# Attention in a two-layer hybrid trunk: the halves of a head's output are copied by ScalarE, and added and split for a pair of heads by POOL

## The chip, the cores and the metric

The kernel runs on one core of one Trainium2 chip. The metric is the device time of one execution in microseconds (us). TensorE (PE in the profile, PEld for its weight loads), VectorE (DVE), ScalarE (ACT), GpSimd (POOL) and SyncE (SP) each work through a queue of their own in a fixed order, and wait for one another by semaphores.

## The reference

The model has two layers. Each normalises x, projects it once, runs three mixers side by side (sparse attention with 8 heads, gated linear attention, spatial gating), projects their joined outputs back and adds them to x; a SwiGLU block follows. The sequence is 512 long, the width 1024, a head 64 wide, and everything is in float32. What matters here is the attention mixer:

```python
s = jnp.einsum('bqghd,bcgd->bghqc', qb, kc)                 # 31 compressed blocks
p_cmp = masked_softmax(s, cmp_end <= t)
o_cmp = jnp.einsum('bghqc,bcgd->bqghd', p_cmp, vc)
...
p = masked_softmax(einsum(qb, ksel), tok <= t)              # selected blocks
o_slc = einsum(p, vsel)
...
p = masked_softmax(einsum(qb, kwb), wmask)                  # window
o_win = einsum(p, vwb)
return gb[..., 0:1] * o_cmp + gb[..., 1:2] * o_slc + gb[..., 2:3] * o_win
...
x = x + jnp.concatenate([o_nsa, o_gla, o_sg], axis=-1) @ w_out[l]
```

With 512 positions, 8 blocks of 64 and up to 16 chosen, the second term takes every block, and the window of 512 takes every earlier position. Both are causal attention over the whole sequence, with keys and values of their own.

## The kernel before

To keep float32 precision on matmuls of a rounded type, the kernel splits a value into a high half (the value rounded to that type) and a low half (the rest). A product is then two or three matmuls. Weights are split as they arrive (`w_split`, L318 on ScalarE, L321 on VectorE), tiles read from PSUM or SBUF in `split_psum` (L299 on ScalarE for the high half, L300 on VectorE for the low one).

`mixer` holds a layer's attention. It loops over four pairs of heads (`hp`, from L1188), the two heads of a pair (`hh`), and two branches (`br`: selected and window). For a branch and each of four blocks of 128 queries, TensorE forms scores (L1215, L1216, L1234, L1235), VectorE takes the row maximum (L1218, L1237), and ScalarE the exponential with its row sum (L1222, L1239). The four tiles of P are 128, 256, 384 and 512 columns wide. VectorE turns the sums and the gates into a factor `rr` (L1244, L1245). Then P is scaled by it: the first two tiles on VectorE (L1253), the third on ScalarE (L1251), and the fourth on POOL (L1249), which by a written dependency waits for VectorE's scaling. TensorE transposes P (L1262) in three groups (columns 0, 1, and 2 with 3 of the key blocks); each group is copied out of PSUM as a high and a low half, PT (L299, L300), and multiplied by V (L1275 for the high half of PT, L1276 for the low).

The weights of that last product, `vst`, hold V's high half in 64 columns and its low half in the other 64. So the accumulator O, one PSUM bank of 128 rows by 512 queries, has in 64 rows the product with V's high half and in the other 64 that with V's low half. Both branches and the compressed term (L1286, L1287) add into it, and the head's output is the sum of the two halves of rows. That bank is the only one of its kind (`rings["o"]`), so the first L1275 of the next head waits until O has been read.

At the end of a head, ScalarE copies one half of O to `oc` (L1288), shifted by 64 rows where the half lies in the other half's place, and VectorE adds the other half to it straight from PSUM (L1289). After the second head `oc` has a pair's 128 rows, and `split_psum` makes from it the high and low half that the output projection reads (`kt`, L299 and L300). `oc` comes from a ring of six buffers named tmp.

Nothing in the code writes out the queue order of these steps. A scheduler sets it from the order in the code, from priorities (`tc.high_priority`), and from its own estimate of when inputs are ready. It runs a head's score matmuls and exponentials ahead of the previous head's end. It also fills TensorE's queue within attention with the first half of the output projection (`out_proj` with k0=4, L336 to L338), which needs the other two mixers only.

Of the kernel before, what the change touches and what calls it, by code (L numbers as in the profile page):

```python
# [10 lines left out]
F32 = mybir.dt.float32  # L11
# [5 lines left out]
ALU = mybir.AluOpType  # L17
# [10 lines left out]
H = 8  # L28
# [115 lines left out]
def trunk_kernel(ctx: ExitStack, tc: tile.TileContext, a, out):  # L144
    nc = tc.nc
# [9 lines left out]
    def nm(s):  # L155
        uid[0] += 1
        return f"{s}_{uid[0]}"
# [7 lines left out]
    def psum(tag):  # L165
        taken[tag] += 1
        return banks[:, rings[tag][(taken[tag] - 1) % len(rings[tag])], :]
# [130 lines left out]
    def split_psum(hi, lo, src):  # L298
        nc.scalar.copy(hi, src)  # L299
        nc.vector.tensor_tensor(lo, src, hi.bitcast(F32), op=ALU.subtract)  # L300
# [266 lines left out]
    def mixer(l, norm, xkt, eu=None):  # L567
# [65 lines left out]
        with tc.tile_pool(name=f"mx{l}", bufs=1, reuse_waits="tile") as mp:  # L633
            def tmp(n=SEQ, dt=F32):
                return mp.tile([P, SEQ], dt, tag="tmp", name=nm("tmp"), bufs=6)[:, 0:n]
# [11 lines left out]
            with tc.tile_pool(name=f"ma{l}", bufs=1, reuse_waits="tile") as ap:  # L647
# [29 lines left out]
                for lp in range(2):  # L677
                    hs = slice(64 * lp, 64 * lp + 64)
# [4 lines left out]
                for w_i in range(2):  # L683
                    pa = pos_t(w_i, l).rearrange("p (s a) -> p a s", s=2)
                    for s in range(2):
                        hi, lo = (kvR[w_i][:, :, 65 * s : 65 * s + 1, h] for h in range(2))
# [374 lines left out]
            with tc.tile_pool(name=f"mt{l}", bufs=1, reuse_waits="tile") as tp_:  # L1061
# [20 lines left out]
                for g in range(G):  # L1082
                    for b in range(2):
                        prep_k(g, b)
                    hi = km2[g][64:128].rearrange("p b (n c) -> p b n c", c=P)
# [99 lines left out]
                def load_q(h):  # L1185
                    (nc.gpsimd.tensor_copy if h > 1 else nc.scalar.copy)(qm1[h % GH][0:64], qst[h // GH][0:64, h % GH, :])

                for hp in range(H // 2):  # L1188
                    if hp % 2 == 0:
                        okt[hp // 2] = kt_tile()  # L1190
                    kt = okt[hp // 2]
                    oc = tmp()
                    for hh in range(2):
                        h = 2 * hp + hh
                        g, h4 = h // GH, h % GH
# [5 lines left out]
                        O = psum(OT[h % len(OT)])  # L1201
                        first = True
                        for br in range(2):
# [43 lines left out]
                            for i in SORD:  # L1247
# [4 lines left out]
                                else:  # L1252
                                    scaled = nc.vector.tensor_scalar(ps_[i], ps_[i], rr[:, i : i + 1], None, op0=ALU.mult)  # L1253

                            tc.add_manual_dep(p3.ins, scaled.ins.name, mybir.DependencyInfo(mybir.DependencyClass.Sync, mybir.DependencyReason.DATA),
                                              reason="port")
                            for js in JG:
                                T = psum(TT[js[0]])
                                c = 0
# [24 lines left out]
                        hs = slice(64 * hh, 64 * hh + 64)  # L1284
# [1 line left out]
                        nc.tensor.matmul(O, lhs, pcT[g][0], start=False, stop=False)  # L1286
                        nc.tensor.matmul(O, lhs, pcT[g][1], start=False, stop=True)  # L1287
                        nc.scalar.copy(oc[hs, :], O[ls, :])  # L1288
                        nc.vector.tensor_tensor(oc[hs, :], oc[hs, :], O[hs, :], op=ALU.add)  # L1289
                    split_psum(kt[:, hp % 2, 0, :], kt[:, hp % 2, 1, :], oc)  # L1290
            return okt

    def out_proj(l, okt, k0, kts, nrm, tags=None):
# [413 lines left out]
```

## Time and profile before

| | us |
|---|---|
| median of 3 runs | 1287.74 (1286.69 to 1287.77) |
| the profiled execution | 1286.52 |
| its span, first to last instruction | 1284.7 |
| attention, layer 0 | about 176 to 276 |
| attention, layer 1 | about 806 to 906 |

One execution is profiled on the chip. A row of a group of instructions names the line, the engine, the operation, output and input by the program's names, partitions x elements, the count, the busy time and the mean duration in ns, and the idle time of the engine just before them with what ended it. Matmuls overlap in their pipeline, so a busy PE is not PE at its peak. The rows that carry the argument stand in the prediction.

### The profile page before, as it was taken

Reading aid. Unit: us, or ns where it says so; the run is one execution under the profiler, and the core shown is the slowest. Engines: PE = TensorE matmul, PEld = TensorE weight load, DVE = VectorE, ACT = ScalarE, POOL = GpSimd, SP = SyncE. Lnnn points to the kernel's source line nnn. Section 1 sums busy time; section 2 is a strip of 40 time slices with the busy share of each in tenths; the row PEclk is TensorE's granted clock in tenths of the full one; section 3 lists DMA queues with packets and bytes.
Section 4 is the critical chain, followed back from the end, with each engine's and each line's share of the span. In section 5 each row is a group of like instructions: output and inputs, shape, how many; then the busy total and the mean of one; then the engine's idle time right before and its main releaser. Section 6 shows DMA issues by size and latency. Waiting matters only on the chain. (4 is left out here: it accounts for less than half of the span.)

```text
span 1284.7 us, 18046 instructions
## 1 busy us (share of the span) xinstructions
PE 1257.3 (98%) x6678; PEld 1038.5 (81%) x6678; DVE 918.2 (71%) x1645; ACT 677.0 (53%) x1288; POOL 160.5 (12%) x157
## 2 busy tenths in 40 slices
PE   8999999999999999999999999999999999999997
PEld 7888788778888888888888877777788888888886
DVE  6767799977856775587446678998767457827775
ACT  6675367864533553354346733788544445515532
POOL 0101222122000100010301012121210001000102
PEclk9999999999999999999999999999999999999999
DMA  6451441034335885483434317210533448754811
GB/s 231 142 180 34 115 108 33 17 87 127 98 105 141 197 232 146 111 200 99 115 94 149 116 34 175 64 33 3 146 98 99 131 117 210 216 130 133 227 66 66
DMA packets 134204, 155.01 MB, mean 121 GB/s; under 512 B 9307, under 2 KB 86885, under 8 KB 134117
## 3 DMA queue, kind: packets, MB, share of 16 engines
q1 hardware_dynamic: 117392, 128.81, 33.3%
q0 software_dynamic: 10208, 20.84, 9.2%
q10 hardware_dynamic: 6516, 4.22, 1.5%
q8 instruction: 52, 0.85, 0.3%
q14 instruction: 36, 0.29, 0.1%
HBM read 149.92 MB, written 2.10 MB: 118 GB/s over the span
## 5 line engine op out<-in xcount | busy, mean ns | idle before, releaser
L318 ACT CAST hl<-raw 128x1024 fp32r<-128x1024 f32 (+3 forms) x170 | 175.2, 1035 | 226.5 <-PE banks L338 160.9
L321 DVE TENSOR_TENSOR hl<-raw,hl 128x1024 fp32r<-128x1024 f32 (+3 forms) x170 | 207.1, 1222 | 94.6 <-ACT hl L318 93.0
L336 PE MATMUL banks<-hl,kt 128*128 128x512 f32 (+2 forms) x688 | 257.9, 375 | 1.1 <-ACT hl L318 1.1
L337 PE MATMUL banks<-hl,kt 128*128 128x512 f32 (+2 forms) x688 | 256.4, 373 | 0.0
L338 PE MATMUL banks<-hl,kt 128*128 128x512 f32 (+2 forms) x688 | 256.1, 373 | 0.0
L337 PE MATMUL banks<-kt,hl 128*128 128x512 f32 x384 | 151.5, 394 | 0.0
L338 PE MATMUL banks<-kt,hl 128*128 128x512 f32 x384 | 151.1, 394 | 0.0
L336 PE MATMUL banks<-kt,hl 128*128 128x512 f32 x384 | 150.4, 394 | 0.0
L336 PEld LDWEIGHTS banks<-hl,kt 128*128 128x128 f32 x688 | 129.5, 188 | 23.6 <-ACT hl L318 1.9
L337 PEld LDWEIGHTS banks<-hl,kt 128*128 128x128 f32 x688 | 129.5, 188 | 21.8 <-DVE hl L321 0.3
L338 PEld LDWEIGHTS banks<-hl,kt 128*128 128x128 f32 x688 | 129.4, 188 | 21.7
L318 ACT CAST hl<-wx 128x1024 fp32r<-128x1024 f32 x48 | 50.5, 1052 | 79.8 <-PE banks L338 69.1
L337 PEld LDWEIGHTS banks<-kt,hl 128*128 128x128 f32 x384 | 72.2, 188 | 14.7 <-DVE kt L295 0.9
L338 PEld LDWEIGHTS banks<-kt,hl 128*128 128x128 f32 x384 | 72.3, 188 | 13.7
L336 PEld LDWEIGHTS banks<-kt,hl 128*128 128x128 f32 x384 | 72.0, 188 | 13.3 <-ACT kt L299 0.3
L321 DVE TENSOR_TENSOR hl<-wx,hl 128x1024 fp32r<-128x1024 f32 x48 | 58.7, 1224 | 18.4 <-ACT hl L318 18.2
L500 DVE TENSOR_TENSOR xT<-xT,banks 128x512 f32<-128x512 f32 x56 | 37.5, 681 | 47.6 <-PE banks L338 47.6
L337 PE MATMUL banks<-act,hl 128*128 128x512 f32 x172 | 67.0, 390 | 0.0
L338 PE MATMUL banks<-act,hl 128*128 128x512 f32 x172 | 66.9, 389 | 0.0
L336 PE MATMUL banks<-act,hl 128*128 128x512 f32 x172 | 66.9, 390 | 0.0
L300 DVE TENSOR_TENSOR PT<-banks,PT 128x384 fp32r<-128x384 f32 (+1 forms) x96 | 54.6, 597 | 14.1 <-ACT PT L299 13.2
L336 PE MATMUL banks<-hl,act 128*128 128x512 f32 (+1 forms) x164 | 63.0, 384 | 0.0
(356 smaller groups left out, 2404.1 us busy)
## 6 DMA issues: line engine op xcount, KB each, us to landing
raw<-in_w_gate_dram SPq DMA_DIRECT2D x44, 512.0 KB, 3.9
raw<-in_w_up_dram SPq DMA_DIRECT2D x44, 512.0 KB, 4.0
raw<-in_w_in_dram SPq DMA_DIRECT2D x32, 512.0 KB, 3.7
raw<-in_w_down_dram SPq DMA_DIRECT2D x36, 256.0 KB, 4.0
raw<-in_w_down_dram SPq DMA_DIRECT2D x18, 512.0 KB, 3.7
raw<-in_w_out_dram SPq DMA_DIRECT2D x16, 512.0 KB, 4.3
raw<-in_cmp_w_k_dram SPq DMA_DIRECT2D x8, 512.0 KB, 3.9
raw<-in_cmp_w_v_dram SPq DMA_DIRECT2D x8, 512.0 KB, 4.9
```

The lines of the kernel that those rows point to most:

```text
L300: nc.vector.tensor_tensor(lo, src, hi.bitcast(F32), op=ALU.subtract)
L318: last_cast[:] = [nc.scalar.copy(hl[:, 0, 0:n], raw[:, 0:n])]
L321: e_.tensor_tensor(hl[:, 1, 0:n], raw[:, 0:n], hl[:, 0, 0:n].bitcast(F32), op=ALU.subtract)
L336: nc.tensor.matmul(ps, lh, rh, start=start, stop=False, skip_group_check=skip)
L337: nc.tensor.matmul(ps, lh, rl, start=False, stop=False, skip_group_check=skip)
L338: return nc.tensor.matmul(ps, ll, rh, start=False, stop=stop, skip_group_check=skip)
L500: nc.vector.tensor_tensor(xT[:, m, :], xT[:, m, :], ps, op=ALU.add)
```

## The change

For the first three pairs of heads of each layer, VectorE no longer takes part in the end of a head. ScalarE copies both halves of O, one to `oc` and one to a second tile `od` of the same ring. When the pair is complete, its join is put on a list; it is taken from there after the scaling of P in the next pair's first branch, as the code is written. A join is three instructions: POOL adds `od` to `oc`, ScalarE casts the high half, POOL subtracts to get the low half. The last pair is left as it was (there `od` is `oc`). Line numbers grow by 7 behind L1187, by 8 behind L1192, and by 10 behind L1256, so L1249 becomes L1257, L1251 becomes L1259 and L1288 becomes L1298.

```diff
+                joins = []
+
+                def join(hi, lo, oc, od):
+                    nc.gpsimd.tensor_tensor(oc, oc, od, op=ALU.add)
+                    nc.scalar.copy(hi, oc)
+                    nc.gpsimd.tensor_tensor(lo, oc, hi.bitcast(F32), op=ALU.subtract)
+
                 for hp in range(H // 2):
...
                     oc = tmp()
+                    od = tmp() if hp < H // 2 - 1 else oc
                     for hh in range(2):
...
                                               reason="port")
+                            if joins:
+                                join(*joins.pop())
                             for js in JG:
...
                         nc.scalar.copy(oc[hs, :], O[ls, :])
-                        nc.vector.tensor_tensor(oc[hs, :], oc[hs, :], O[hs, :], op=ALU.add)
-                    split_psum(kt[:, hp % 2, 0, :], kt[:, hp % 2, 1, :], oc)
+                        if od is oc:
+                            nc.vector.tensor_tensor(oc[hs, :], oc[hs, :], O[hs, :], op=ALU.add)
+                        else:
+                            nc.scalar.copy(od[hs, :], O[hs, :])
+                    if od is oc:
+                        split_psum(kt[:, hp % 2, 0, :], kt[:, hp % 2, 1, :], oc)
+                    else:
+                        joins.append((kt[:, hp % 2, 0, :], kt[:, hp % 2, 1, :], oc, od))
```

VectorE has 18 instructions fewer in the whole program, and POOL 12 more. ScalarE has 12 more, TensorE and SyncE as many as before. Three places of the queues follow, each in layer 0; layer 1 has the same order there. The names carry the buffers' numbers, and the brackets name the engines whose semaphores an instruction waits for.

The first place is ScalarE's queue at the end of the first pair. Here tmp is `oc` or `od`, PT the high half of a transposed group of P, kt the high half for the output projection, and P with rr the scaling of the 384-wide tile. Before:

```order
L1125 CAST qst_1805<-banks 64x512 [waits DVE_49]
L1251 ACTIVATE P_2186<-P_2186,rr_2194 128x384 [waits DVE_49,Activation_49]
L1288 COPY tmp_1807<-banks 64x512 [waits PE_49]
L299 CAST PT_2159<-banks 128x512 [waits PE_49]
L299 CAST PT_2167<-banks 128x384 [waits DVE_49,PE_49]
L299 CAST kt_1806<-tmp_1807 128x512 [waits DVE_49]
L1146 COPY tmp_2228<-banks 128x256 [waits PE_49]
```

With the change:

```order
L1125 CAST qst_1805<-banks 64x512 [waits DVE_49]
L1298 COPY tmp_1807<-banks 64x512 [waits PE_49]
L1302 COPY tmp_1808<-banks 64x512
L299 CAST PT_2162<-banks 128x512 [waits PE_49,Activation_49]
L299 CAST PT_2170<-banks 128x384 [waits DVE_49,PE_49]
L1192 CAST kt_1806<-tmp_1807 128x512 [waits Pool_49]
L1259 ACTIVATE P_2189<-P_2189,rr_2197 128x384 [waits DVE_49]
L1146 COPY tmp_2231<-banks 128x256 [waits PE_49]
```

A second copy stands behind the first, the cast of kt waits for POOL, and the scaling of P, ahead of the copy before, now stands behind that cast.

The second place is POOL's queue there. P with rr is the scaling of the 512-wide tile, and qm a copy of queries. Before:

```order
L1249 TENSOR_TENSOR P_2146<-P_2146,rr_2148 128x512 [waits DVE_49,PE_49,Activation_49]
L1186 COPY qm_186_1602<-qst_1805 64x512 [waits Activation_49]
L1249 TENSOR_TENSOR P_2192<-P_2192,rr_2194 128x512 [waits DVE_49,PE_49,Activation_49]
L1186 COPY qm_187_1603<-qst_1805 64x512 [waits PE_49,Activation_49]
L1249 TENSOR_TENSOR P_2297<-P_2297,rr_2299 128x512 [waits DVE_49,Activation_49]
```

With the change:

```order
L1257 TENSOR_TENSOR P_2146<-P_2146,rr_2148 128x512 [waits DVE_49,PE_49,Activation_49]
L1186 COPY qm_186_1602<-qst_1805 64x512 [waits Activation_49]
L1191 TENSOR_TENSOR tmp_1807<-tmp_1807,tmp_1808 128x512 [waits Activation_49]
L1257 TENSOR_TENSOR P_2195<-P_2195,rr_2197 128x512 [waits DVE_49,PE_49,Pool_49]
L1193 TENSOR_TENSOR kt_1806<-tmp_1807,kt_1806 128x512 [waits Activation_49]
L1186 COPY qm_187_1603<-qst_1805 64x512 [waits PE_49]
```

With the change, a little later in the same queue, at the second pair's join:

```order
L1257 TENSOR_TENSOR P_2475<-P_2475,rr_2477 128x512 [waits DVE_49,PE_49,Activation_49]
L1191 TENSOR_TENSOR tmp_2107<-tmp_2107,tmp_2108 128x512 [waits Activation_49]
L1193 TENSOR_TENSOR kt_1806<-tmp_2107,kt_1806 128x512 [waits Activation_49]
L1257 TENSOR_TENSOR P_2544<-P_2544,rr_2546 128x512 [waits DVE_49,PE_49,Activation_49]
```

At the first join the add stands ahead of a scaling of P and the subtraction behind it; at the second, both stand ahead of the next scaling.

The third place is ScalarE's queue at the end of the fifth head. Before:

```order
L1222 ACTIVATE P_2643,den_2629<-banks,nmx_2641 128x256 [waits DVE_49]
L1288 COPY tmp_2386<-banks 64x512 [waits PE_49]
L299 CAST PT_2552<-banks 128x512 [waits PE_49]
L299 CAST PT_2560<-banks 128x384 [waits PE_49,Activation_49]
L1251 ACTIVATE P_2579<-P_2579,rr_2587 128x384 [waits DVE_49,Activation_49]
```

With the change:

```order
L299 CAST PT_2557<-banks 128x512 [waits DVE_49,PE_49]
L1230 ACTIVATE P_2640,den_2633<-banks,nmx_2636 128x128 [waits DVE_49]
L1230 ACTIVATE P_2646,den_2632<-banks,nmx_2644 128x256 [waits DVE_49]
L1298 COPY tmp_2387<-banks 64x512 [waits PE_49]
L1302 COPY tmp_2388<-banks 64x512
L299 CAST PT_2565<-banks 128x384 [waits PE_49,Activation_49]
L1259 ACTIVATE P_2584<-P_2584,rr_2592 128x384 [waits DVE_49]
```

The first cast of PT has moved from behind the copy to a place ahead of both.

## The prediction

> **What bounds the kernel now.** I read the busy line of the page first, then the attention stage of layer 0 cut into three stretches, then who makes TensorE's weight loads wait there.
>
> ```profile
> PE 1257.3 (98%) x6678; PEld 1038.5 (81%) x6678; DVE 918.2 (71%) x1645; ACT 677.0 (53%) x1288; POOL 160.5 (12%) x157
> ```
>
> Over the whole program TensorE is the bound, and work moved between VectorE, ScalarE and POOL can only win where TensorE waits for them. The change lies in the attention stage, which runs twice: about 176 to 276 us in layer 0 and 806 to 906 us in layer 1. In the windows the columns are the stretch, its length, and the busy time of PE, PEld, DVE, ACT and POOL.
>
> ```profile
> 176.00:190.00 14.00, 13.47 (x80) 11.06 (x79) 12.92 (x30) 10.61 (x32) 1.65 (x2) 1.00 0.16 48
> 190.00:250.00 60.00, 57.99 (x330) 46.43 (x329) 56.87 (x132) 49.18 (x135) 12.79 (x14) 1.00 0.09 27
> 250.00:276.00 26.00, 23.21 (x131) 17.47 (x129) 20.52 (x49) 19.97 (x55) 7.68 (x8) 1.00 0.17 47
> 820.00:880.00 60.00, 57.99 (x331) 46.55 (x330) 56.86 (x132) 49.19 (x135) 12.38 (x14) 1.00 0.10 28
> ```
>
> From 190 to 250 VectorE is busy for 56.87 of 60 us (95%), ScalarE for 49.18 (82%), POOL for 12.79 (21%). The last row is the same stretch of layer 1, alike to 0.02 us, so every term counts twice. The granted clock is 1.00 in all four. PE's 57.99 hides waits, because a matmul's record is longer than its share of the engine:
>
> ```profile
> 223.71 0.39 PE L337 MATMUL banks<-kt,hl 128*128 128x512 f32 x1
> 223.94 0.40 PE L338 MATMUL banks<-kt,hl 128*128 128x512 f32 x1
> ```
>
> These records last 0.39 us, but the next starts after 0.23. Waits are better read at the weight loads (176 to 276 us; us in total, times, longest):
>
> ```profile
> PEld banks L1275 <- ACT PT L299: 7.3, 17, 1.2
> PEld banks L1276 <- DVE PT L300: 3.6, 9, 0.9
> PEld banks L1262 <- POOL P L1249: 2.6, 6, 0.8
> ```
>
> So some 13.5 us of a layer's 100 are TensorE waiting for ScalarE's high halves of P transposed (7.3), VectorE's low halves (3.6) and POOL's scaling (2.6). About 27 us in both layers is the ceiling of any gain. VectorE is the fullest of the three and feeds the others, but ScalarE's cast is most often what ends last.
>
> **The change, part by part.** *VectorE loses work.*
>
> ```profile
> L1289 DVE TENSOR_TENSOR tmp<-tmp,banks 64x512 f32<-64x512 f32 x16 | 10.9, 684 | 6.5 <-ACT tmp L1288 6.1
> L300 DVE TENSOR_TENSOR kt<-tmp,kt 128x512 fp32r<-128x512 f32 x8 | 5.5, 688 | 1.4 <-ACT kt L299 1.4
> ```
>
> Three of four pairs change in each of two layers: 12 adds of 0.684 us (8.2) and 6 subtractions of 0.688 us (4.1) go, 12.3 us in all. In layer 0's full stretch (190 to 250) lie four adds and two subtractions: 2.7 + 1.4 = 4.1 us.
>
> *ScalarE gains 12 copies* of 64x512; the high halves stay on it.
>
> ```profile
> L1288 ACT COPY tmp<-banks x16: 578/581/587, 199.5 to 911.0; 64x512 f32<-64x512 f32 x16
> 199.50 0.58 ACT L1288 COPY tmp<-banks 64x512 f32<-64x512 f32 x1 [0.56 <-PE banks L1287]
> 200.10 0.58 ACT L1125 CAST qst<-banks 64x512 fp32r<-64x512 f32 x1
> 200.59 0.58 ACT L299 CAST PT<-banks 128x512 fp32r<-128x512 f32 x1
> ```
>
> A record is 0.58 us, but a second one of that size, back to back, costs 0.49 (200.10 to 200.59). I take 0.5: 3.0 us a layer, 2.0 in the full stretch. The single output bank is freed about as soon as before: a 0.58 copy and a 0.68 add ran one after the other; two copies take 1.1.
>
> *POOL gains 12 instructions* of 128x512 with two full operands. Attention shows none; the nearest are the norm's sums and POOL's scaling, whose second operand is one column.
>
> ```profile
> L353 POOL TENSOR_TENSOR nacc<-nacc,nsq x21: 1283/1397/1852, 289.0 to 938.8; 128x512 f32<-128x512 f32 x21
> L1249 POOL TENSOR_TENSOR P<-P,rr x32: 1039/1040/1043, 183.3 to 902.0; 128x512 f32<-128x512 f32 x32
> ```
>
> The price is 1.04 to 1.85 us each; I take the undisturbed 1.28, since the norm's sums are the same operation. That is 15.4 us, 7.7 a layer, against some 78 us of idle POOL in the layer's 100. Throughput is no question; position is.
>
> *The added waits.* ScalarE's high half now waits for POOL's add and stands two casts of PT behind the copies (first of the places shown with the change). These casts take about 1.0 us:
>
> ```profile
> 214.46 1.08 ACT L299 CAST PT<-banks 128x512 fp32r<-128x512 f32 x2
> 215.44 0.62 ACT L299 CAST kt<-tmp 128x512 fp32r<-128x512 f32 x1
> ```
>
> So ScalarE stands still some 1.28 - 1.0 = 0.3, with the signals 0.4 us, at each of three joins; bounds are 0 (a 1.04 us add) and 0.9 (1.85). Behind it in its queue stands the scaling of the 384-wide P, which a transpose needs. On POOL, the scaling of the 512-wide P stands behind the add (first join) or the subtraction (second and third).
>
> ```profile
> 213.87 1.04 POOL L1249 TENSOR_TENSOR P<-P,rr 128x512 f32<-128x512 f32 x1 [1.33 <-ACT P L1251]
> 213.86 0.58 ACT L1288 COPY tmp<-banks 64x512 f32<-64x512 f32 x1
> 216.75 0.82 PE L1262 MATMUL banks<-ident,P 128*128 128x128 f32 x6
> ```
>
> At the first join POOL scaled from 213.87 to 214.91. Now both copies end at about 213.86 + 1.1 = 214.95, the add at 216.2, the scaling at 217.3. TensorE transposed that tile in the group of six that began at 216.75, its last member about 0.5 us in. The 2.3 us of slack is used up, but hardly exceeded: I charge nothing, and up to 1 us for the range. The next join should be as near.
>
> *The port.* DVE instructions with two SBUF operands wait for POOL:
>
> ```profile
> 269.81 1.04 POOL L1249 TENSOR_TENSOR P<-P,rr 128x512 f32<-128x512 f32 x1 [7.55 <-ACT P L1239]
> 269.98 0.89 DVE L1245 TENSOR_TENSOR rr<-rr,gates 128x4 f32<-128x4 f32 x1
> L1245 DVE TENSOR_TENSOR rr<-rr,gates x32: 93/160/892, 181.9 to 900.4; 128x4 f32<-128x4 f32 x32
> L1245 DVE TENSOR_TENSOR rr<-rr,gates 128x4 f32<-128x4 f32 x32 | 8.6, 268 | 0.3
> ```
>
> The 128x4 product needs 0.16 us; begun inside POOL's 1.04 us it took 0.89 and ended with it (270.87, 270.85). The code keeps its own scaling clear of VectorE's by a written dependency; the joins have none. If half of the POOL instructions catch one such product or weight subtraction, at 0.64 us (half of 1.28), that is 0.32 each: 1.3 us for the four in the full stretch; bounds 0 and 5.1 (four times 1.28). The Trainium skill ("SBUF — State Buffer", section "Who interferes with whom") says that the port pair shared by VectorE and GpSimd is an exclusive lock held for the whole instruction by whichever began first, also against a VectorE instruction with two SBUF inputs. The trace agrees, with the 0.89 above.
>
> *The sum.* In the full stretch VectorE is relieved of 4.1 - 1.3 = 2.8 us. ScalarE rises from 49.18 by 2.0 and two waits of 0.4 to 52.0, VectorE falls from 56.87 to 54.1: VectorE stays the fullest, but by 2 us only, so I let two thirds reach the path: 1.9 us a layer. Outside the stretch the sooner freed bank (0.2 us) and a join's wait (0.4) cancel. Both layers: 3.8 us. The order also shifts filler matmuls of the output projection; their number is unchanged, and I price that at 0. The profiled execution took 1286.52 us (span 1284.7 and 1.8 around it); it becomes 1282.7. The median of the three runs, 1287.74, lies 1.22 higher, so the forecast is **1283.9**.
>
> **The rivals.** 1. *ScalarE becomes the bound (slower).* TensorE's largest wait, 7.3 us, is for casts of PT, and the change puts a copy (0.49) in front of such a cast after five or six heads of a layer, and a wait for POOL (0.4) at three joins: 6 x 0.49 + 3 x 0.4 = 4.1 us. If these casts end the waits, that lands on the path and only the 1.9 us above stands against it: +2.2 us a layer, **1292.1**. It decides when the second PT cast, not the low half on VectorE, ends last. For it: 7.3 against 3.6. Against: for the fifth head the built order now puts a PT cast ahead of the copies (third place shown with the change).
>
> 2. *The port gives it back (no change).* If each of the 12 POOL instructions costs VectorE 0.64, 7.7 of 12.3 us return; of the 4.6 left, under half lay in the full stretch as net relief (1.9 of 6.2 us reached the path above), so 1.4 us: **1286.3**. For it: the 0.89. Against: median L1245 is still 0.16, so most of them miss POOL's existing 16 instructions a layer. The Trainium skill ("Perfetto Trace Analysis", section "Optimizing Scalar/DVE Operations") warns that because GPSIMD and DVE share an SBUF read port, moving work between those two might not help. By that rule the outcome is this rival; the trace shows the lock, but also adds from PSUM that it does not touch.
>
> 3. *All of VectorE's relief arrives.* If every one of 12.3 us shortens the stage, **1275.4**; more likely two thirds, 8.2 us: **1279.5**. For it: VectorE at 95%. Against: ScalarE at 82% before it gains work.
>
> **How the numbers follow.** Forecast case (2.6 to 7 us faster) 0.46; rival 3 beyond 7 us 0.08; rival 2 and everything else within 0.2% 0.25; rival 1 0.21. 0.2% is 2.6 us, about what a measurement of this kernel tells from no change. Faster 0.54, same 0.25, slower 0.21. The range takes in rival 3's two thirds with the port free (another 2 us) and rival 1 at its price: 1277.5 to 1292.5.
>
> **What would show it.** In the changed profile: VectorE's busy time down by 9 to 12 us, ScalarE's up by about 7, POOL's up by 15 to 20; the same stretch two to three us shorter in each layer; TensorE's wait for VectorE's PT below 3.6 us. The added POOL rows should read about 1.28 us, and ScalarE's high half should show idle time of 0.3 to 0.5 before it, released by POOL. The forecast is wrong if TensorE's waits for ScalarE's PT or for POOL's scaled P rise by more than 2 us a layer (rival 1), or if VectorE's 128x4 products grow from a mean of 0.27 to 0.6 us (rival 2).

## The result and the profile after

| | us | ratio to the kernel before (95%) |
|---|---|---|
| before, median | 1287.76 (1286.69 to 1288.59, 4 runs) | |
| after, median | 1296.07 (1295.29 to 1296.3, 4 runs) | 1.0064 (1.0046 to 1.0081) |
| after, repeated beside later experiments | 1296.37 (1296.14 to 1297.56, 5 runs) | 1.0073 (1.0060 to 1.0085) |

The change made the kernel 8.3 us slower; 1283.9 was forecast. The profiled execution after took 1296.3 us (span 1294.5). Here are the busy line of its page, the same windows as before (the third ends 4 us later, since attention does), and what TensorE's weight loads wait for in layer 0's attention:

```profile
PE 1261.0 (97%) x6678; PEld 1041.8 (80%) x6678; DVE 909.8 (70%) x1627; ACT 683.5 (53%) x1300; POOL 178.1 (14%) x169
```

```profile
176.00:190.00 14.00, 13.47 (x77) 10.81 (x77) 12.70 (x26) 10.58 (x29) 2.25 (x3) 1.00 0.23 73
190.00:250.00 60.00, 55.23 (x312) 44.10 (x311) 52.91 (x120) 49.53 (x134) 17.66 (x17) 1.00 0.10 28
250.00:280.00 30.00, 27.66 (x148) 21.85 (x148) 21.46 (x55) 24.13 (x65) 9.21 (x9) 0.94 0.11 36
820.00:880.00 60.00, 55.76 (x314) 44.33 (x312) 53.49 (x123) 47.57 (x127) 16.33 (x17) 1.00 0.12 35
```

```profile
PEld banks L1285 <- ACT PT L299: 5.3, 11, 1.7
PEld banks L1286 <- DVE PT L300: 3.2, 6, 1.2
PEld banks L1272 <- POOL P L1257: 2.7, 5, 0.8
PEld banks L336 <- ACT kt L1192: 1.9, 2, 1.6
PEld banks L1285 <- ACT tmp L1302: 1.3, 2, 0.8
```

VectorE was relieved: 56.87 us of the full stretch became 52.91. But in the same 60 us TensorE got through 312 matmuls in place of 330. The total of its waits for PT even fell; new ones stand beside them (kt, and tmp, the second copy), and the longest grew from 1.2 to 1.7 us.

How late the program is can be read from lines that have the same matmuls in both kernels. L1077's first and last matmuls come ahead of attention in layer 0 and in layer 1, L359's behind it (minimum, median and longest duration in ns, then the first and last start in us); before, then after:

```profile
L1077 PE MATMUL banks<-ident,tmp x32: 270/272/328, 150.0 to 786.6; 128*128 128x128 f32 x32
L359 PE MATMUL banks<-cf,nacc x24: 170/250/250, 311.5 to 942.6; 128*128 128x1 f32 x24
```

```profile
L1077 PE MATMUL banks<-ident,tmp x32: 270/272/332, 151.5 to 793.7; 128*128 128x128 f32 x32
L359 PE MATMUL banks<-cf,nacc x24: 170/250/250, 317.0 to 952.5; 128*128 128x1 f32 x24
```

The program after is 1.5 us late ahead of attention, 5.5 behind it, 7.1 ahead of layer 1's attention and 9.9 behind it. So attention costs **4.0 us in layer 0 and 2.8 in layer 1** (the starts are rounded, so each figure holds to 0.1 us), and 1.6 us are lost between the two. The first 1.5 belong to the start of the run: kernels below that take as long as the one before show 1.2 to 1.3 there as well (runs 6 and 11).

Three places in each layer explain most of the new waits. *The first join* (a row's start and duration in us, then engine, line and tiles; in brackets idle time and what ended it):

```profile
216.40 1.58 DVE L1261 TENSOR_SCALAR P<-P,rr 128x128 f32<-128x128 f32 x2
216.56 1.27 POOL L1191 TENSOR_TENSOR tmp<-tmp,tmp 128x512 f32<-128x512 f32 x1 [2.07 <-ACT tmp L1302]
218.01 1.16 DVE L300 TENSOR_TENSOR PT<-banks,PT 128x512 fp32r<-128x512 f32 x2
218.75 0.50 PE L1286 MATMUL banks<-PT,vst 128*128 128x512 f32 x1 [0.64 <-DVE PT L300]
```

VectorE's two scalings of P took 1.58 us, since POOL's sum began between them; the second, which took 0.35 us before, took 1.38 and ended at 217.98, just behind the sum (216.56 + 1.27 = 217.83). The low half of PT came late, and TensorE stood 0.64 us.

*The second join*, at the fourth head's end:

```profile
241.96 0.62 ACT L1259 ACTIVATE P<-P,rr 128x384 f32<-128x384 f32 x1 [0.16 <-DVE rr L1253]
242.59 0.58 ACT L1298 COPY tmp<-banks 64x512 f32<-64x512 f32 x1
243.18 0.58 ACT L1302 COPY tmp<-banks 64x512 f32<-64x512 f32 x1
243.78 0.58 ACT L299 CAST pcT<-banks 128x512 fp32r<-128x512 f32 x1
244.26 0.59 ACT L299 CAST PT<-banks 128x512 fp32r<-128x512 f32 x1
244.91 0.50 PE L1285 MATMUL banks<-PT,vst 128*128 128x512 f32 x1 [1.37 <-ACT PT L299]
```

Before, one copy stood in front of these two casts and the scaling behind them. Now a scaling and two copies stand in front, and TensorE waits 1.37 us. The starts also give the price of a copy in the queue: the second starts 0.59 us behind the first, and the cast 0.60 behind the second, while a cast starts 0.48 behind a cast.

*The third join.* TensorE's queue, before and after, around the first matmul of the output projection that reads the third pair's kt:

```
L1235 MATMUL banks<-km_183_1599,qm_187_1603 128x384
L336 MATMUL banks<-kt_2385,hl_2995 128x512
L1276 MATMUL banks<-PT_2686,vst_275 128x256 [waits DVE_49]
```

```
L1285 MATMUL banks<-PT_2684,vst_275 128x384 [waits Activation_49]
L336 MATMUL banks<-kt_2386,hl_3001 128x512 [waits Activation_49]
L1286 MATMUL banks<-PT_2684,vst_275 128x384 [waits DVE_49]
```

Before, the high half of that kt had been ready for 2.1 us (its cast ended at 262.92, the matmul began at 265.00). Now the matmul waits for a cast that waits for POOL:

```profile
266.85 1.27 POOL L1191 TENSOR_TENSOR tmp<-tmp,tmp 128x512 f32<-128x512 f32 x1
268.15 0.62 ACT L1192 CAST kt<-tmp 128x512 fp32r<-128x512 f32 x1 [0.79 <-POOL tmp L1191]
268.83 0.50 PE L336 MATMUL banks<-kt,hl 128*128 128x512 f32 x1 [1.35 <-ACT kt L1192]
```

And behind this wait the windows (the last three columns are granted clock, DMA share, GB/s) show something that no part of the prediction had:

```profile
268.00:269.00 1.00, 0.17 (x1) 0.17 (x2) 0.04 (x1) 0.84 (x2) 0.27 (x2) 1.00 0.00 0
269.00:270.00 1.00, 1.00 (x8) 0.96 (x9) 0.00 (x0) 1.00 (x4) 1.00 (x1) 0.87 0.00 0
270.00:271.00 1.00, 1.00 (x6) 1.00 (x6) 0.00 (x0) 1.00 (x5) 0.14 (x1) 0.50 0.00 0
271.00:272.00 1.00, 1.00 (x6) 1.00 (x5) 0.18 (x1) 0.93 (x2) 0.00 (x0) 0.50 0.00 0
272.00:273.00 1.00, 1.00 (x4) 0.81 (x3) 0.87 (x2) 0.00 (x0) 0.00 (x0) 0.50 0.00 0
273.00:274.00 1.00, 1.00 (x5) 0.79 (x5) 1.00 (x4) 0.08 (x1) 0.00 (x0) 0.93 0.00 0
```

For 3.4 us (three windows at 0.50 and 0.26 + 0.14 us of their neighbours) TensorE ran at half its clock.

### The profile page after: what moved, and what is told of

It reads as the page before. It is cut to its first block, busy times and chain, and to the rows that moved or that the text cites. A ratio compares the mean times of both kernels' runs of the same rounds, so it can differ in the third digit from the quotient of the medians.

```text
span 1294.5 us, 18040 instructions
## 1 busy us (share of the span) xinstructions
PE 1261.0 (97%) x6678; PEld 1041.8 (80%) x6678; DVE 909.8 (70%) x1627; ACT 683.5 (53%) x1300; POOL 178.1 (14%) x169
## 4 chain that ended last, share of the span: by engine, by line
PE 78%; DVE 9%; ACT 6%; issue 3%; DMA 2%; POOL 1%; ACTq 0%; POOLq 0%; DVEq 0%
PE banks L336 22%; PE banks L337 21%; PE banks L338 21%; PE banks L1272 2%; DMA raw<-in_w_in_dram 1%; ACT hl L318 1%; PE banks L1285 1%; PE banks L1286 1%; DVE hl L321 1%; PE banks L471 1%; DVE PT L300 1%; PE banks L1615 1%; POOL P L1257 1%; PE banks L969 1%; DVE w1h L743 1%
## 5 line engine op out<-in xcount | busy, mean ns | idle before, releaser
L318 ACT CAST hl<-raw 128x1024 fp32r<-128x1024 f32 (+3 forms) x170 | 175.2, 1034 | 222.1 <-PE banks L338 166.6
L336 PE MATMUL banks<-hl,kt 128*128 128x512 f32 (+2 forms) x688 | 258.0, 375 | 1.4 <-ACT hl L318 1.4
L336 PE MATMUL banks<-kt,hl 128*128 128x512 f32 x384 | 152.0, 398 | 2.8 <-ACT kt L1192 2.7
L336 PEld LDWEIGHTS banks<-hl,kt 128*128 128x128 f32 x688 | 129.4, 188 | 23.8 <-ACT hl L318 2.2
L318 ACT CAST hl<-wx 128x1024 fp32r<-128x1024 f32 x48 | 50.5, 1052 | 79.7 <-PE banks L338 70.7
L336 PEld LDWEIGHTS banks<-kt,hl 128*128 128x128 f32 x384 | 72.3, 189 | 17.4 <-ACT kt L1192 3.8
L336 PE MATMUL banks<-act,hl 128*128 128x512 f32 x172 | 66.9, 390 | 0.0
```

The lines of the kernel that those rows point to most:

```text
L318: last_cast[:] = [nc.scalar.copy(hl[:, 0, 0:n], raw[:, 0:n])]
L336: nc.tensor.matmul(ps, lh, rh, start=start, stop=False, skip_group_check=skip)
```

## The experiments

A filler here is a matmul of the output projection that stands within attention; `kk` numbers the pair of heads whose part of kt it reads. Theories: **A**, the filler that waits at the third join; **B**, the port at the first; **C**, the second copies on ScalarE; **D**, POOL; **E**, single long waits and the half clock behind some of them; **F**, ScalarE's load bounds the stage. G, H and W come with their runs. Each kernel was timed 4 to 11 times; the table at the end has all of them.

**1. The filler later.** Edit to the changed kernel (`pv` is the first product with V of the seventh head's second branch):

```diff
-                    mm3(ps, ...)
+                    with tc.issue_after(pv.ins) if (k0, kk) == (0, 2) else contextlib.nullcontext():
+                        mm3(ps, ...)
```

> The changed kernel, with one thing altered: the three matmuls of the output projection that read the third pair's part of kt first (L336, L337, L338 with kk = 2) stand in TensorE's queue behind the first product with V of the seventh head's second branch. Only TensorE's queue differs. Theory A (a filler matmul stands too early and waits for the join): in the changed kernel TensorE's queue stood still 1.35 us in front of that L336 (its weight load 1.60) in layer 0 and as long in layer 1, and matmuls behind it were slow in layer 0 (about 1.2 us). So the time falls by 3 to 4.5 us, from 1296.1 to 1291.6 to 1293, and TensorE's waits for ScalarE's kt (1.9 us in the stage) fall below 0.5. Theory B (the port at the first join) and theory C (the second copies): under 1 us of change, since the copies, the sums and VectorE's rows are as before.

1294.01 us, ratio 1.0052 (1.0040 to 1.0064): 2.1 to 2.4 less than the changed kernel, under what A asked for. The wait for kt is gone and none above 0.64 us took its place there; the half clock behind it is gone from layer 0. In layer 1 there is one (at 868), behind a wait of 0.86 us at another place. How much of the gain is the wait itself is not shown: the traced execution is 2.3 us shorter than that of the changed kernel, but 1.6 of this lies ahead of attention (L1077 begins at 149.9, not 151.5), and attention differs by 0.2 in both layers together (6.6 against 6.8, with one stretch at half clock in each).

**2. The copies alone.**

```diff
-                        joins.append((kt[:, hp % 2, 0, :], kt[:, hp % 2, 1, :], oc, od))
+                        nc.vector.tensor_tensor(oc, oc, od, op=ALU.add)
+                        split_psum(kt[:, hp % 2, 0, :], kt[:, hp % 2, 1, :], oc)
```

> Only the first part of the change: ScalarE copies both halves of six heads a layer, but VectorE adds the pair's two tiles at once (one 128x512 add in SBUF in place of two 64x512 adds from PSUM) and does the subtraction. POOL gets nothing and no join is put off. Theory C (the second copies on ScalarE cost the time): 1294 to 1297, near the changed kernel, with TensorE's waits for ScalarE as long as there. Theories A and B (the join's place and POOL): 1285 to 1289, near the kernel before, since VectorE is relieved of six adds of 0.69 us in each two layers against 12 copies of 0.5 us on ScalarE.

1291.06 us, 1.0029 (1.0016 to 1.0041), between the two forecasts: 40% of the loss is there without POOL and without a join put off.

**3. The join on VectorE.** In `join`, `nc.gpsimd` becomes `nc.vector` twice.

> The changed kernel with the join's sum and subtraction on VectorE (0.7 us each by the rows of the kernel before) in place of POOL (1.28 each); copies, and the place of the join in the code, as in the change. Theory A in its narrow form (the join is put off in the code, and so late, whoever does it): TensorE still waits for kt at the third join, 1293 to 1296. Theory D (it is POOL: twice as long, last in its queue, and the port): the high half of kt comes 0.6 us sooner and the low half 1.2, the scheduler's places for the filler matmuls may go back, and the time is 1286 to 1290.

1292.58 us, 1.0036 (1.0023 to 1.0049), between the two forecasts; TensorE no longer stands for kt at the third join, so A in its narrow form is out. Putting the join off costs 1.5 us over run 2 by the medians, but the times of the two runs overlap (1290.14 to 1293.49 against 1289.91 to 1293.28). Giving it to POOL costs the other 3.5 to 3.8, and there no times overlap.

**4. POOL's sum behind VectorE's scaling.** `add` is the sum, `scaled` VectorE's last scaling of the next branch:

```diff
...
+                            elif added:
+                                tc.add_manual_dep(added.pop().ins, scaled.ins.name, mybir.DependencyInfo(mybir.DependencyClass.Sync, mybir.DependencyReason.DATA),
+                                                  reason="port")
```

> The changed kernel, with a written dependency that lets POOL's sum of the first join begin only when VectorE has scaled its tiles of P for the second branch of the third head. POOL's sum waits for one instruction more, and the third tile's scaling on ScalarE now stands ahead of the cast of kt; nothing else moves. Theory B (in the changed kernel the sum, begun at 216.56, held VectorE's 256-wide scaling until 217.83: that took 1.38 us in place of 0.35, and TensorE then stood 0.64 us for VectorE's low half of PT): the scaling is back at 0.35 us, that wait goes, and both layers gain 1.3 to 2 us: 1294 to 1294.8. Theories A and C: within 0.7 us of the changed kernel, because the wait moves to the sum, which then starts 0.4 us later.

1293.86 us (1291.89 to 1298.07), 1.0055 (1.0040 to 1.0070). The wait at the first join is gone. VectorE's 32 scalings of 256 columns are busy for 11.1 us, against 13.2 in the changed kernel (means of 346 and 412 ns); the 2.1 us are the two that had caught a sum. By the medians the kernel is 2.2 to 2.5 us faster than the changed one, a little more than B said, but its six times spread over 6.2 us. The profiled run was the slowest of six; its trace has four stretches at half clock in attention, and its mean granted clock is 0.993, against 0.994 to 0.997 in the other five.

**5. The scaling behind the copies** at the fourth head's end:

```diff
+                                    with tc.issue_after(copied.ins) if (h, br) == (4, 1) else contextlib.nullcontext():
...
```

> The changed kernel, with the scaling of the third tile of P for the fifth head's second branch put behind ScalarE's two copies at the end of the fourth head. There the changed kernel has in ScalarE's queue: scaling (0.62), copy, copy (0.58 each), pcT, PT, and TensorE stood 1.37 us for that PT (244.91); the kernel before had one copy, pcT, PT. Theory E (what the change costs is single long waits of TensorE, and behind some of them 3.4 us at half the granted clock): the wait falls by 0.6 to about 0.75 us, 0.6 a layer, and the stretches at half clock behind that place (1.7 us each, in one layer or the other) go: 1293 to 1295, from 1296.1. Theory F (only the second copies' throughput counts, since ScalarE has become the bound): no change, 1295.5 to 1296.5, because ScalarE does the same work and TensorE waits as long somewhere later.

1292.5 us, 1.0033 (1.0020 to 1.0045): 3.6 less than the changed kernel, more than E asked for and nothing that F allows at this place. The wait of 1.37 us became three:

```profile
245.58 0.50 PE L1286 MATMUL banks<-PT,vst 128*128 128x512 f32 x1 [0.89 <-ACT PT L299]
246.73 0.50 PE L336 MATMUL banks<-kt,hl 128*128 128x512 f32 x1 [0.66 <-ACT kt L1192]
248.08 0.50 PE L337 MATMUL banks<-kt,hl 128*128 128x512 f32 x1 [0.52 <-POOL kt L1193]
```

**6. A wait alone.** In the kernel before, POOL copies a tile of P onto itself twice ahead of its scaling.

> The kernel before, with two copies of a 128x512 tile of P onto itself on POOL ahead of its scaling, once in each layer (first branch of the sixth head); no other queue changes. By the 605 ns of a 64x512 copy on POOL, each takes 0.6 to 1.2 us, and TensorE, whose transposes waited 0.15 us for that tile, waits 1.2 to 2.2 us longer there. If a wait costs itself alone (theory W): 1287.6 plus 2.4 to 4.4 us, mean granted clock 0.997 as before. If the clock is halved for 3.4 us behind a wait of over 1.2 us (theory E): up to 1.7 us more for each layer in which that happens, 1291 to 1295, windows at half clock right behind the waits, and a mean clock of 0.994 to 0.996. If the stage absorbs it (TensorE has other work later): under 1 us.

1287.77 us, ratio 1.0000 (0.9991 to 1.0009). It tells nothing on W (a wait costs its own length) or E: the copies took 0.61 us each, POOL still stood idle for 1.42 us behind them until VectorE's rr was there, and TensorE never stood 0.5 us for that tile.

**7. The low half alone on POOL,** in the kernel before:

```diff
...
+                    (nc.gpsimd if hp < H // 2 - 1 else nc.vector).tensor_tensor(lo, oc, hi.bitcast(F32), op=ALU.subtract)
```

> The kernel before, with one part of the change alone: for the first three pairs POOL subtracts to get the low half of kt, at the end of the pair, as the code is written. ScalarE's copies, VectorE's adds from PSUM and the cast of the high half stay. VectorE loses 6 subtractions of 0.69 us, POOL gains 6 of 1.28, ScalarE nothing. Theory C (the second copies in front of ScalarE's casts are what the change cost, by 0.49 each): 1285.5 to 1288, as before or a little faster, no wait of TensorE above 0.8 us. Theory D (POOL in this place costs by itself): 1289 to 1292, with TensorE's waits for VectorE's PT or POOL's P longer by 1 us a layer.

1289.1 us, 1.0009 (1.0000 to 1.0018), at the lower end of D's range: 4.1 us less work on VectorE, and no gain. TensorE's waits for POOL's P rose as D had it, from 2.6 to 3.9 us in layer 0 (176 to 290 us). A wait of 1.35 us for an exponential on ScalarE is new (230.38, in both layers), though no edit touched it.

**8. The three cures together** (runs 1, 4 and 5).

> The changed kernel with three edits together: the filler matmul of the third pair later (it gave 2.1 us alone), POOL's sum of the first join behind VectorE's scaling (2.2 alone), and the scaling behind the copies at the fourth head. Theory E (the cost lies in these few waits and the half clock behind them): they add up, 1289 to 1291.5, mean clock 0.997, no wait of TensorE above 0.9 us in the stage. Theory F (ScalarE's extra copies bound the stage): 1292 to 1294, not below the better of the single cures by more than 1 us.

1292.99 us, 1.0032 (1.0019 to 1.0045). As F had it: no better than the best of them alone. Two stretches at half clock in layer 0, one in layer 1, behind waits of 0.53 and 0.86 us, or 0.90, 0.66 and 0.52, close together.

**9. The copies added, nothing taken away,** in the kernel before:

```diff
...
                         nc.scalar.copy(oc[hs, :], O[ls, :])
+                        if hp < H // 2 - 1:
+                            nc.scalar.copy(od[hs, :], O[hs, :])
```

> The kernel before with the second copies added and nothing taken away: for six heads a layer ScalarE also copies the other half of O to a tile that nothing reads; VectorE's adds from PSUM and the subtractions stay as they were. ScalarE gains 12 x 0.49 = 5.9 us and VectorE loses nothing. Theory C (the copies cost the change its time, in front of casts that TensorE waits for): 1291 to 1294, 3.4 us or more above the kernel before, since the copies alone with VectorE relieved gave 1291.06. If VectorE's relief was worth two thirds of its size, as the prediction had it (4.1 us of relief in the run with the copies alone, 2.7 of it on the path), it must be 2.7 slower than that one: 1293.8. If the relief was worth nothing: 1291, the same as that one. Theory D (POOL and the place of the join are the cost): 1288 to 1289.

1296.35 us, 1.0074 (1.0061 to 1.0086): as much as the change loses, without POOL and without any join. It lies above every forecast. But one price here is not in the change: VectorE's add from PSUM begins behind the second copy in all 12 of these heads (in ten that copy is what ends its wait), so O's bank is held for two copies and an add. TensorE's waits for that add (176 to 280 us), in the kernel before, in this one and in run 15:

```profile
PE banks L1275 <- DVE tmp L1289: 0.8, 1, 0.8
PE banks L1276 <- DVE tmp L1292: 1.9, 3, 0.9
PE banks L1276 <- DVE tmp L1292: 0.8, 1, 0.8
```

Run 2 is 5.3 us faster. It has 4.1 us less on VectorE, but it also frees the bank without an add and has one stretch at half clock fewer, so the 5.3 are not the price of the relief alone.

**10. The changed kernel once more.**

> The changed kernel once more, beside the others of this chip, to see which parts of its trace recur. Expected: 1295.5 to 1296.5; TensorE's waits of 1.35 us for PT at the fourth head's end and for kt at the third join come back in both layers, to 0.05 us; the stretches at half clock come back at other places or in another number (0 to 4 in the stage, theory E), since the trace of the changed kernel had one behind a wait in layer 0 and none behind the same wait in layer 1.

1296.37 us. The waits came back to 0.02 us (1.39, 1.34, 1.38 and 1.33), the stretches at half clock elsewhere: at 235 and 870, none behind the third join, and again one at 706.

**11. The whole split on POOL,** in the kernel before:

```diff
...
+                    if hp < H // 2 - 1:
+                        nc.gpsimd.tensor_copy(hi, oc)
+                        nc.gpsimd.tensor_tensor(lo, oc, hi.bitcast(F32), op=ALU.subtract)
...
```

> The kernel before with the whole split of kt on POOL for the first three pairs, at the pair's end: POOL casts the high half (a 64x512 cast took it 605 ns, so 0.6 to 1.2 us) and subtracts (1.28). ScalarE loses 6 casts of 0.49 (2.9 us), VectorE 6 subtractions of 0.69 (4.1); nobody gains but POOL. Theory F (ScalarE's share is what counts in this stage, VectorE's is not): 1285 to 1287, faster than the kernel before by 0.5 to 3 us. Theory G (the stage is held by single waits whose places the scheduler deals anew with every edit; relief of an engine does not show): 1288 to 1290, as with the low half alone (1289.1).

1287.25 us, 0.9999 (0.9990 to 1.0008): neither forecast, and no gain from 2.9 us less on ScalarE and 4.1 less on VectorE. TensorE's waits from 176 to 290 us, before and here:

```profile
PEld banks L1275 <- ACT PT L299: 7.6, 18, 1.2
...
PEld banks L1262 <- POOL P L1249: 2.6, 6, 0.8
...
PEld banks L1234 <- ACT P L1239: 0.4, 2, 0.2
```

```profile
PEld banks L1275 <- ACT PT L299: 5.2, 16, 0.6
PEld banks L1262 <- POOL P L1249: 4.0, 8, 0.8
...
PEld banks L1234 <- ACT P L1239: 2.0, 2, 1.8
```

The wait for PT fell by 2.4 us, and two other kinds took over: 1.4 more for POOL's P, and 1.6 more for the exponential of P on ScalarE.

**12. The join's cast on POOL too,** in the changed kernel: `nc.scalar.copy(hi, oc)` becomes `nc.gpsimd.tensor_copy(hi, oc)`.

> The changed kernel with the high half of the join cast by POOL too, so that ScalarE neither casts it nor waits for POOL's sum: ScalarE loses 6 casts (2.9 us) and 6 waits (0.48 each, 2.9 us by the changed kernel's rows), and POOL's join gets 0.6 to 1.2 us longer. If ScalarE's wait for POOL stood on the path at each join: 1290 to 1293. If the late kt is what TensorE waits for (theory A): 1296 to 1299, for kt then comes 0.5 us later still. If ScalarE's two copies are all that matters (theory C): 1294 to 1296.

1301.63 us, 1.0112 (1.0098 to 1.0125), worse than even A had it. ScalarE is relieved of the cast and of its wait, but kt comes later: TensorE's waits for it (L336) are 2.9 us in layer 0, against 1.9 in the changed kernel, and the longest 2.2.

**13. Run 11, with a weight cast later.** There a cast of weights (L318) stood ahead of the exponential that TensorE waited for; `tc.issue_after` puts it behind.

> The kernel with the whole split of kt on POOL, and one cast of a weight block (hl, L318, for the fourth block of the output projection's second half) put behind the exponential of the fourth head's 512-wide P. There that kernel's TensorE stood 1.35 us in both layers: the cast (1.05 us) stood ahead of the exponential in ScalarE's queue and itself waited 0.73 us for a matmul. If relief of ScalarE and VectorE shows as soon as no single wait of this length is left (theory G, first half): the wait goes in both layers and the time falls by 1.5 to 2.7 us, to 1284.5 to 1286, faster than both kernels. If the stage's TensorE work is what is left (its records fill it but for waits under 0.8 us) or the scheduler makes another wait of it: 1286.5 to 1288.

1287.03 us, 1.0002 (0.9993 to 1.0011). The wait of 1.35 us went; attention got 0.5 and 0.3 us shorter than in run 11, not 1.35, and the trace has a stretch at half clock at 700. No faster kernel came of it.

**14. The second pair's fillers later too,** on top of run 8 (the edit of run 1 for `kk` 1 and 2).

> The changed kernel with the three edits of before and one more: the second pair's filler matmuls (kk = 1), too, stand behind the first product with V of the second branch of the head after next. With the three edits TensorE still stood 0.89 for PT, 0.66 for kt and 0.52 for its low half within 3.4 us at the second join, and the clock was halved behind it in one layer. Theory E (waits, and half clock behind those that crowd into one window): the two waits for kt go (1.2 us in each layer, 2.4 in all), at most one stretch at half clock is left in a trace, and the time is 1289 to 1291, from 1292.99. Theory F (ScalarE's copies bound the stage): 1292 to 1293.5, since the waits turn up behind PT.

1293.23 us, 1.0047 (1.0033 to 1.0061): as F had it. No stretch at half clock in the trace up to the run's end, 0.998 mean clock in all five timed runs, no wait for kt of 0.5 us or more, and still 6.0 us above the kernel before. Its waits (176 to 280) and its delay ahead of and behind attention:

```profile
PEld banks L1292 <- ACT PT L299: 9.7, 17, 1.2
PEld banks L1295 <- DVE PT L300: 4.2, 10, 1.2
```

```profile
L1079 PE MATMUL banks<-ident,tmp x32: 270/272/328, 151.5 to 790.9; 128*128 128x128 f32 x32
L359 PE MATMUL banks<-cf,nacc x24: 170/250/250, 315.9 to 949.4; 128*128 128x1 f32 x24
```

TensorE's wait for ScalarE's PT rose to 9.7 us. Attention is 2.9 and 2.5 us longer than before (4.4 - 1.5, 6.8 - 4.3).

**15. The load without the place.** As run 9, but the six extra copies a layer read queries, not O:

```diff
-                            nc.scalar.copy(od[hs, :], O[hs, :])
+                            nc.scalar.copy(od[0:64, :], qst[g][0:64, h4, :].bitcast(F32))
```

> As the kernel with the copies added, which took 1296.35, but the six extra copies a layer read a 64x512 tile of queries that has long been ready, not O. ScalarE's added work is the same in number and size (nothing reads the result). What changes: no copy waits for the end of a head's products or holds the output bank, and the scheduler puts three of the six a layer somewhere else in ScalarE's queue, while three still stand right behind the copy of O. If ScalarE's load alone is the price (theory F): 1295 to 1297, as there. If it is the place, in front of the casts of PT at a head's end, and the hold of the bank (theory H): half or less of the 9.0 us, 1289 to 1292.

1292.93 us, 1.0041 (1.0027 to 1.0055), between F and H. Attention is 2.5 and 2.7 us longer, with no half clock in it; six copies at 0.5 to 0.6 us are 3.0 to 3.5. Run 9 had 5.0 in each layer. Of the 2.3 to 2.5 between the two, 1.1 is the hold of the bank (1.9 against 0.8 in the rows under run 9), and one stretch at half clock in each layer, at 1.0 to 2.1 us by the table below, would be the rest. What the place of the copies costs was not told apart: three of the six still stand behind the copy of O.

All runs: time above the kernel before of the same set, then from each trace the delay of attention in the layers (as worked out above, from L1077 and L359 or the lines that they became), what was lost between, and in parentheses the stretches at half clock in that part:

| run | us above before | layer 0 | between | layer 1 |
|---|---|---|---|---|
| changed kernel | 8.3 | 4.0 (1) | 1.6 (1) | 2.8 (0) |
| 10 the same again | 9.1 | 3.8 (1) | 1.0 (1) | 3.9 (1) |
| 1 filler later | 6.4 | 2.8 (0) | 1.2 (1) | 3.8 (1) |
| 2 copies alone | 3.5 | 1.1 (0) | -0.2 (0) | 3.2 (1) |
| 3 join on VectorE | 5.0 | 2.5 (1) | -0.3 (0) | 3.0 (1) |
| 4 sum behind scaling | 6.3 | 5.3 (2) | -0.5 (0) | 5.0 (2) |
| 5 scaling behind copies | 4.4 | 2.9 (1) | -0.4 (0) | 1.9 (0) |
| 6 wait alone | -0.3 | 0.3 (0) | -0.1 (0) | 0.2 (0) |
| 7 low half on POOL | 1.0 | 1.3 (0) | -0.3 (0) | 1.0 (0) |
| 8 three cures | 4.9 | 3.7 (2) | -0.5 (0) | 2.3 (1) |
| 9 copies added | 9.0 | 5.0 (1) | -0.2 (0) | 5.0 (1) |
| 11 split on POOL | -0.1 | 0.1 (0) | -0.2 (0) | -0.2 (0) |
| 12 cast on POOL | 14.3 | 6.6 (1) | 1.1 (1) | 6.7 (1) |
| 13 split, weight cast later | -0.2 | -0.4 (0) | 1.1 (1) | -0.5 (0) |
| 14 fillers behind | 6.0 | 2.9 (0) | -0.1 (0) | 2.5 (0) |
| 15 copies of queries | 5.5 | 2.5 (0) | 1.2 (1) | 2.7 (0) |

Where one kernel's layers differ by one stretch, that layer is longer by 1.2 (changed kernel), 1.0 (run 1), 2.1 (run 2), 1.0 (run 5) and 1.4 us (run 8); between the layers a stretch goes with 1.0 to 1.6 us, where the rest have -0.5 to -0.1.

## Why the prediction was wrong

Four kernels stand in a row: the copies with nothing taken away, 9.0 us slower than the kernel before (run 9); the two adds replaced by one in SBUF, 3.5 slower (run 2); the join put off, 5.0 (run 3, not clear of run 2); POOL in VectorE's place, 8.3 to 9.1 (the change). So **ScalarE's copies lose time by themselves**: 5.5 us where they do not hold the bank (run 15), and still 3.5 with VectorE relieved. **POOL's part in the join costs 3.5 to 3.8 us more.** With one or more of its long waits put right (runs 5, 8 and 14) the time is 1292.5 to 1293.2, which is that of run 3. The shares hold for this order of steps: POOL without the second copies cost 1.0 us or nothing (runs 7 and 11), and no run put a join off without the copies. Neither E nor F holds alone: run 5 gained more than F allows, runs 8 and 14 less than E asks.

By the steps of the prediction:

- *VectorE loses work.* Nearly: its busy time went from 918.2 to 909.8 us over the program, 8.4 less, where 9 to 12 were named.
- *The fullest engine; two thirds of its relief reach the path.* **This step failed.** It compared busy sums (VectorE 54.1 after the change, ScalarE 52.0) and let the fullest decide. ScalarE's added work so entered the sum only as the third that was held back. The runs show most of it on the path: six more copies on ScalarE, 3.0 to 3.5 us, made attention 2.5 to 2.7 us longer though VectorE was the fuller engine (run 15). VectorE's relief, priced at 1.9 us a layer, was worth nothing alone (run 7, and run 11 with ScalarE relieved as well). Why relief of ScalarE, too, buys nothing in the kernel before is shown only in part: other waits took its place (run 11), and with the longest of them gone the time stayed (run 13).
- *ScalarE's 12 copies at 0.5 us.* The price was a little low: the 0.49 was read from a cast to a cast, while the copy in the line above it takes 0.60 (199.50 to 200.10), and the second copies start 0.59 us behind the first (all 12, to 0.01), which makes up to 3.5 us a layer, not 3.0. Attention got 2.5 to 2.9 us longer in runs 14 and 15, which have no half clock there; where VectorE is relieved and no join is put off, the one layer without half clock got 1.1 us longer (run 2, layer 0).
- *The bank freed about as soon.* Nearly: TensorE's waits for the second copy are 1.3 us in layer 0.
- *POOL's durations.* Right: 1.27 and 1.29 us for the sum and the subtraction (1.28 said). That the join costs little beyond them was wrong: 3.5 to 3.8 us from run 3 to the change. *ScalarE's wait for POOL*: 0.4 said, 0.48 measured (2.9 us over six). *POOL's scaling behind the join, charged nothing*: right, 2.7 us of waits against 2.6.

```profile
L1191 POOL TENSOR_TENSOR tmp<-tmp,tmp 128x512 f32<-128x512 f32 x6 | 7.6, 1270 | 4.5 <-ACT tmp L1302 4.5
L1193 POOL TENSOR_TENSOR kt<-tmp,kt 128x512 fp32r<-128x512 f32 x6 | 7.7, 1286 | 2.9 <-ACT kt L1192 2.9
L1192 ACT CAST kt<-tmp 128x512 fp32r<-128x512 f32 x6 | 3.7, 618 | 2.9 <-POOL tmp L1191 2.9
```

- *The port at 0.32 for each POOL instruction, on instructions with two SBUF operands.* Its sum for VectorE was 3.8 us and 2.1 are seen, on another kind of instruction: a scaling whose second operand is one column, held for 1.04 us in each layer; and 2.6 us were won on the 128x4 products, which met POOL less often than before. The Trainium skill ("SBUF — State Buffer", section "Who interferes with whom") says that tensor_scalar can enter modes that use the shared port pair, and then contends as well; the trace agrees, with 1.39 us for one of 0.35.
- *The fillers, priced at 0.* **Wrong too:** their number is unchanged, but one now waits 1.35 us in each layer. Putting it later gave 2.1 to 2.4 us by the medians, of which attention in the traces shows 0.2 (run 1).
- *Rival 1, ScalarE's casts.* It had the direction, and its price, 2.2 us a layer, is near the 2.5 to 2.9 of run 14. Its sign to look for, a rise of TensorE's waits for PT by over 2 us, does not show in the changed kernel (5.3 against 7.3), only where the fillers' waits are out of the way (9.7 in run 14). So its mechanism is borne out there, and for the changed kernel itself it is argued. Rival 2's 128x4 products got shorter, not longer (268 to 185 ns), and rival 3 is out.
- *No step spoke of the clock.* With 5.4 us for attention from run 14, one stretch at half clock in attention (1.2) and one between the layers (1.7, 1.6 against -0.1), the sum is 8.3 us, what was measured. That it fits so well is luck in part: it is worked out from two traces, and the stretch between the layers also came in run 13, which is as fast as the kernel before.

## What to carry to other kernels

Ask of each instruction that is moved in whose queue it will stand, and in front of what, before any busy share is added up: copies of about half a microsecond on an engine with 18% to spare made attention longer by nearly their sum (run 15), though another engine was fuller. Look through the bound engine's own queue, too, for filler work whose input the change makes later. And judge an edit in the kernel it is for: POOL's subtraction or its whole split cost 1.0 us or nothing in the kernel before, and POOL's join 3.5 to 3.8 beside the copies.

## What the hardware showed that was not expected

*Half clock behind waits.* In run 4's trace the granted clock steps to one half at 246.2, 270.1, 881.1 and 905.0 us, for 3.413 us each; the first two starts are 7 x 3.413 us apart and the third 186 x 3.413 behind the first. So there is a fixed grid, and TensorE's records leave 1.4 to 1.7 of the 3.41 us ahead of each free. It does not take one long wait (0.53 and 0.86 us sufficed in run 10), nor does each such window lead to it: waits of 1.35 us were without effect in runs 7 and 11. The Trainium skill ("TensorE: Matmul & The Clock Gate", section "What's actually happening") describes a free-running window of 3413 ns and half rate after an idle window; the length and the grid agree with the trace, but here a window idle for a third to a little over half was enough: the 19 stretches in attention, over all traces, stand behind windows of which 1.1 to 1.9 us were free. What decides between 1.1 and 1.6 us of idle time stays open, since windows of both kinds are found there. So does the stretch at about 705 us (6 of 17 traces); in the changed kernel's trace TensorE had not stood at all in the 3.41 us ahead of it.

*Added work in front of a tile that TensorE needs can be free:* 1.2 us more on POOL left the time as it was (run 6), since POOL then stood idle for another 1.42 us.
